# A mixture-of-experts stage on one core: first w1 pieces of the next expert ahead of w2, the first group gathered whole, the last expert in full rows

## The chip, the cores and the metric

The kernel runs on one core of one Trainium2 chip. The metric is device time in microseconds: the median of three runs. A separate execution was taken with the hardware profiler; its span (first to last instruction) and its own time are given below.

## The reference, cut to what matters

One layer of a hybrid backbone over 256 latent tokens of width 1024: modulated norm, one input projection, differential attention and a long convolution, a gated merge, an output projection; then a mixture of 32 experts, of which each token takes 4. The change touches the end of the output projection and the experts:

```python
x_new = x + g1 * merge_branches(oa, ob, gx, *merge_params)
x_new = x_new + g2 * moe_ffn(modulate(x_new, norm2_g[l], sh2, sc2), *moe_params)

# moe_ffn: route, then for each block of rows of one expert e
logits = (xt @ router_w + router_b)
top_v, top_i = lax.top_k(logits, 4)
wts = softmax(top_v)
gu = xblk @ w1[e] + b1[e]               # w1[e]: 1024 x 2048
gate, up = split(gu, 2)
gate = min(gate, 7); up = clip(up, -7, 7)
act = (up + 1) * gate * sigmoid(1.702 * gate)
y = act @ w2[e] + b2[e]                 # w2[e]: 1024 x 1024, added with wts to its tokens
```

All weights are float32: an expert is 8 MB of w1 and 4 MB of w2, the 32 experts 403 MB, of 467 MB that the DMA queues move.

## The kernel before, in words

**Loads.** All weights go through one list of loads of 1 MiB (`want`), in the order of use, each into one of 25 slots of 8 KB per partition (`NS`). SyncE issues the next load when a slot is free and the number of loads held is under a bound; the bound follows a table of steps (`ROOM`), where a step is any taking or giving back of a slot (`tick`). `done(key)` gives a used piece's slot back. Slots also hold arrays: X (the new rows), XN (their normed rows, split into a high and a low float32r part), RAW (quarters, here the gathered columns of four experts), YS (outputs of two experts), MTh/MTl (the merged branches split in two), PAIR. At the start of the experts 24 loads may be held; then the bound falls to 20.

**Order.** Instructions of each engine run in the order in which the program writes them. In the projections, steps of other work are hung on numbered weight pieces (`TASKS`): `bias_load` and `bias_parts` bring the experts' first bias in and split it (ACT casts, POOL subtractions), `merge_a` writes MTh on ACT and MTl on POOL for the output projection, whose pieces are 96 to 111.

**Between projection and experts.** `new_rows` adds the projection to x (VectorE); `squares` and `rstd` make the norm's factor; `new_columns`, `logits`, `folded`, `top4` and `positions` do the routing. `spin` runs a few idle matmuls.

**Experts.** Slots of 64 rows per expert. `gather(g)` makes the columns of four experts in four steps k2 of two column blocks: a one-hot matrix S (`slots_of`) times both parts of XN, then scale and shift on ACT and VectorE (`modulate_slots`) into RAW. Group 0 is different: `gather_first` makes expert 0 alone from X in float32, one step per piece of w1, so that XN and RAW are allocated after w1 of expert 0; the other three of the group follow after its w2. For each expert `up_bias` starts the two PSUM sums, `up` runs the eight pieces of w1 (four matmuls each, gate and up, two column halves), `hidden` does clamp, sigmoid and product on VectorE and ACT, and `down` transposes the hidden layer, copies it (`at`), runs w2 (four loads), and writes the output in two parts to YS (`yr`, `YS`). Between `up` and the transposes stand `up_bias` of the next expert, on even experts `scatter` of the pair before (one-hot times YS, added to X), at expert 1 `second_bias`, and at the end of each group the next gather and its `weights`.

**The last expert** (31) is loaded in halves of hidden columns: w1 in rows of 256 columns (1 KB), each load of two pieces, w2 in rows of 512 columns. `up_last(q)`, `last_units(q)` and `down_last(q, c)` work half by half; `out_rows` and `scatter_last` write the result by column halves c and row tiles i. The scatter of expert 30 (`last_but_one`), its weights and G2 are hung between pieces (`between`).

Scratch tiles of 2 KB per partition (`t1_tile`) take four tags in turn; one is kept for the second part of the first bias.

Of the kernel before, what the change touches and what calls it, by code (L numbers as in the profile page):

```python
# [20 lines left out]
P = 128  # L21
# [50 lines left out]
    ("bias_load", (), (90,)), ("merge_b", (1, 1), (90,)), ("merge_a", (0, 0), (93, 94)), ("merge_a", (0, 1), (95, 97)), ("bias_parts", (), (99,)),  # L72
# [17 lines left out]
]  # L90

# [62 lines left out]
def tile_kernel(ctx: ExitStack, tc: tile.TileContext, a: dict, out: bass.AP):  # L154
# [140 lines left out]
    for h in range(4):  # L295
        want(("out", h), [P, 2, 1024], a["w_out"][0, h * 256:(h + 1) * 256].rearrange("(k p) n -> p k n", p=P))
        PIECES += [(("out", h), j) for j in range(4)]
    for e in range(NE - 1):
        for k in range(KC):
            want(("w1", e, k), [P, 2048], a["exp_w1"][0, e, k * P:(k + 1) * P, :])  # L300
# [5 lines left out]
    w2 = a["exp_w2"][0, NE - 1].rearrange("(b f p) n -> p b f n", p=P, b=2)  # L306
    for q in range(2):
        for k in range(0, KC, 2):
            want(("w1", NE - 1, q, k), [P, 2, 4, 256], [(j, w1[:, k + j, :, q * 256:(q + 1) * 256]) for j in range(2)])
    for q in range(2):  # L310
        for c in range(2):
            want(("w2", NE - 1, q, c), [P, 2, 2, 512], [(b, w2[:, b, 2 * q:2 * q + 2, c * 512:(c + 1) * 512]) for b in range(2)])
# [83 lines left out]
    T1 = deque(range(4))  # L396

    def t1_tile(shape, name, dt=F32):
        T1.rotate(-1)
        return wk.tile(shape, dt, tag=f"t1{T1[-1]}", name=name, bufs=1)  # L400

# [36 lines left out]
    Z = t1_tile([P, 512], "Z")  # L438
# [7 lines left out]
    cT = t1_tile([P, KC, 32], "cT")  # L446
# [15 lines left out]
    def bias_parts():  # L462
        B1.append(kept([P, 512], "B1", F32R))
        B1.append(t1_tile([P, 512], "B1u", F32R))
        T1.pop()
# [349 lines left out]
    def qk_rope(raw, rstd, gain, rt, nm):  # L815
        r3 = raw.rearrange("p (g f) -> p g f", g=8)
        t1 = t1_tile([P, 512], f"t1{nm}")
# [221 lines left out]
    def pt_out(h, i):  # L1039
        e2 = es.pop((h, i))[0]  # L1040
        if i == 0:
            PTs[h] = [t1_tile([P, 2, T], f"PT{h}{j}") for j in range(2)]
# [264 lines left out]
    def new_rows(i, h):  # L1307
        hs = slice(h * 512, (h + 1) * 512)
        t_ = t1_tile([P, 512], f"og{i}{h}")
# [65 lines left out]
    def up_bias(e, q=""):  # L1375
        g, u = pst(f"ps_eg{e}{q}", True), pst(f"ps_eu{e}{q}", True)
        acts[e, q] = g, u
        cols = slice(0, 512) if q == "" else slice(q * 256, q * 256 + 256)
        for b, ps in ((0, g), (1, u)):
            pe.matmul(ps[:, 0:cols.stop - cols.start], pick, B1[b][:, cols], start=True, stop=False, skip_group_check=True)  # L1380
        if q != 0 and e < NE - 1:
# [3 lines left out]
    for i in range(2):  # L1385
# [5 lines left out]
        if i == 0:  # L1391
            squares(0)
    free.extend(ring)
    tick("arrays", -3)
    release("MTl", "MTh")
    new_columns(0, (act.copy, act.copy))
    spin(SPINS[5])
    new_columns(1, (dve.tensor_copy, act.copy))
    squares(1)
    logits(0)  # L1400
    rstd(0)
# [3 lines left out]
    rstd(1)  # L1405
    for i in range(2):
# [4 lines left out]
    for i in range(2):  # L1411
        positions(i)
    spin(SPINS[8])

    SS, XG, OT = {}, {}, {}
    XN = []


    def rows_parts():
        hi_, lo_ = XN  # L1420
        for i in range(2):
            act.activation(hi_[:, i], X[:, i], AF.Copy, scale=st2[:, i, 5:6])
            dve.scalar_tensor_tensor(lo_[:, i], X[:, i], st2[:, i, 5:6], hi_.bitcast(F32)[:, i], ALU.mult, ALU.subtract)

# [13 lines left out]
    first = []  # L1438

    def gather_first(k):  # L1440
        if k == 0:
            first.extend((t1_tile([P, KC, CAP], "xg0"), pst("ps_xg0", True),
                          wk.tile([P, 2, CAP], F32, tag="hz", name="S0", bufs=3)))
            for i in range(2):
                dve.tensor_scalar(first[2][:, i], iota, pos[:, i, 0:1], st2[:, i, 5:6], ALU.is_equal, ALU.mult)
        xg, ps, s0 = first
        for i in range(2):
            pe.matmul(ps[:, k * CAP:(k + 1) * CAP], X[:, i, k * P:(k + 1) * P], s0[:, i], start=(i == 0), stop=(i == 1))
        modulate_slots(xg[:, k], ps[:, k * CAP:(k + 1) * CAP], k, act if k % 2 else dve)
        XG[0, k] = xg[:, k]  # L1450
        if k == KC - 1:
            unhold("ps_xg0")

    def gather(g):
        n = 4 if g else 3
        for k2 in range(4):
            xg = quarter([P, 2, 4, CAP], F32)
            ps = pst(f"ps_xg{g}_{k2}")
            for kk in range(2):
                k = 2 * k2 + kk  # L1460
                for j, (i, xn) in enumerate((i, xn) for i in range(2) for xn in XN):
                    pe.matmul(ps[:, kk * T:(kk + 1) * T], xn[:, i, k * P:(k + 1) * P],  # L1462
                              SS[g][:, i].rearrange("p e c -> p (e c)"), start=(j == 0), stop=(j == 3))
            for kk in range(2):
                k = 2 * k2 + kk
                modulate_slots(xg[:, kk, 4 - n:4].rearrange("p e c -> p (e c)"), ps[:, kk * T + (4 - n) * CAP:(kk + 1) * T], k, dve if kk else act)
                for e in range(4 - n, 4):
                    XG[4 * g + e, k] = xg[:, kk, e]
# [32 lines left out]
    def up(e):  # L1501
        g, u = acts.pop((e, ""))
        for k in range(KC):
            wt = w(("w1", e, k))
            xg = XG[e, k]
            for b, ps in ((0, g), (1, u)):
                for h in range(2):
                    pe.matmul(ps[64 * h:64 * h + 64, :], xg, wt[:, b * 1024 + h * 512:b * 1024 + (h + 1) * 512],  # L1508
                              start=False, stop=(k == KC - 1), skip_group_check=True)
            done(("w1", e, k))  # L1510
            if e == 0 and k < KC - 2:
                gather_first(k + 2)
# [294 lines left out]
```

## Time and profile before

| | |
|---|---|
| median of three runs | 1273.14 us (1270.09 to 1273.43) |
| profiled execution | 1275.61 us, span 1273.9 us |
| TensorE | 1119.0 us busy (88%), mean granted clock 0.969 of 2.4 GHz |
| VectorE, ACT, POOL | 514.0, 279.3, 167.4 us busy |
| DMA | 467.10 MB, mean 367 GB/s |
| chain that ended last | TensorE 43%, DMA 35%, VectorE 13% |

The page cuts the span into 40 slices of 31.8 us. TensorE's busy share is high nearly everywhere, but its matmuls overlap and their ends are modelled, so that row alone does not say what bounds the kernel; the rows on what the DMA engines moved, and the chain of waits, say more.

### The profile page before, as it was taken

Reading aid. Unit: us, or ns where it says so; the run is one execution under the profiler, and the core shown is the slowest. Engines: PE = TensorE matmul, PEld = TensorE weight load, DVE = VectorE, ACT = ScalarE, POOL = GpSimd, SP = SyncE. Lnnn points to the kernel's source line nnn. Section 1 sums busy time; section 2 is a strip of 40 time slices with the busy share of each in tenths; the row PEclk is TensorE's granted clock in tenths of the full one; section 3 lists DMA queues with packets and bytes.
Section 4 is the critical chain, followed back from the end, with each engine's and each line's share of the span. In section 5 each row is a group of like instructions: output and inputs, shape, how many; then the busy total and the mean of one; then the engine's idle time right before and its main releaser. Section 6 shows DMA issues by size and latency. Waiting matters only on the chain.

```text
span 1273.9 us, 14261 instructions
## 1 busy us (share of the span) xinstructions
PE 1119.0 (88%) x5645; PEld 551.6 (43%) x5645; DVE 514.0 (40%) x817; ACT 279.3 (22%) x506; POOL 167.4 (13%) x152
## 2 busy tenths in 40 slices
PE   7889789998889899989989888888888798879896
PEld 5678678896333433333343224222322332233232
DVE  5699995966222322232323123322312322223232
ACT  5563465753210101011111001111100101111110
POOL 2385454322000000000000000000000000000000
PEclk9999899999889899999989999999999999999999
DMA  9984536878689999999999999999999999999996
GB/s 328 400 289 153 181 130 234 328 303 351 261 319 415 387 384 416 417 418 418 417 417 417 416 417 417 417 417 417 418 417 418 417 417 418 417 418 417 418 371 238
DMA packets 105810, 467.10 MB, mean 367 GB/s; under 512 B 8992, under 2 KB 18188, under 8 KB 71948
## 3 DMA queue, kind: packets, MB, share of 16 engines
q1 hardware_dynamic: 102416, 462.26, 90.8%
q10 hardware_dynamic: 3324, 3.88, 1.0%
q8 instruction: 46, 0.75, 0.2%
q14 instruction: 24, 0.20, 0.0%
HBM read 465.07 MB, written 1.05 MB: 366 GB/s over the span
## 4 chain that ended last, share of the span: by engine, by line
PE 43%; DMA 35%; DVE 13%; ACT 3%; issue 3%; POOL 2%; ACTq 0%; SPq 0%; DVEq 0%; POOLq 0%
PE ps_ey L1540 12%; PE ps_eg L1508 9%; PE ps_eu L1508 9%; PE ps_xg L1462 2%; DMA w____w___22___3__5783<-in_exp_w_dram 2%; DVE AA L643 2%; DMA w____w___16___3__5011<-in_exp_w_dram 2%; DMA w____w___29___3__6656<-in_exp_w_dram 2%; DMA w____w___14___3__4793<-in_exp_w_dram 2%; DMA w___w___29__3__6520<-in_exp_w_dram 2%; DMA w___w___27__3__6302<-in_exp_w_dram 2%; DMA w____w___25___3__6161<-in_exp_w_dram 2%; DMA w___w___15__7__4862<-in_exp_w_dram 2%; DMA w____w___20___3__5506<-in_exp_w_dram 2%; DMA w____w___27___3__6379<-in_exp_w_dram 2%
## 5 line engine op out<-in xcount | busy, mean ns | idle before, releaser
L1520 DVE TENSOR_SCALAR ga<-ps_eg 128x512 f32<-128x512 f32 (+1 forms) x33 | 22.3, 675 | 325.9 <-PE ps_eg L1508 318.4
L481 POOL CAST pick<-both 128x128 fp32r<-128x128 f32 x32 | 24.5, 766 | 862.1 <-PE ps_eu L1380 862.0
L1554 DVE TENSOR_TENSOR yr<-ps_ey,G 64x512 f32<-64x512 f32 x62 | 42.7, 688 | 229.0 <-PE ps_ey L1540 228.3
L1555 ACT ACTIVATE YS<-yr,wsl 64x512 fp32r<-64x512 f32 x62 | 44.6, 719 | 311.8 <-DVE yr L1554 311.8
L1521 ACT ACTIVATE sg<-ga 128x512 f32<-128x512 f32 (+1 forms) x33 | 20.4, 619 | 352.9 <-DVE ga L1520 352.9
L1556 DVE SCALAR_TENSOR_TENSOR YS<-yr,wsl,YS 64x512 fp32r<-64x512 f32 x62 | 46.3, 747 | 48.8 <-ACT YS L1555 48.8
L1462 PE MATMUL ps_xg<-S,XNh 128*128 128x256 f32 x128 | 37.3, 324 | 13.9 <-DVE S L1429 13.9
L1665 DVE TENSOR_TENSOR X<-X,ps_sc 128x512 f32<-128x512 f32 x60 | 37.4, 680 | 3.0 <-PE ps_sc L1663 3.0
L392 PE MATMUL ps_g<-XTh,wsp 128*128 128x256 f32 x128 | 37.9, 296 | 0.0
L393 PE MATMUL ps_g<-XTl,wsp 128*128 128x256 f32 x128 | 36.2, 283 | 0.0
L394 PE MATMUL ps_g<-XTh,wsp 128*128 128x256 f32 x128 | 36.2, 283 | 0.0
L1462 PEld LDWEIGHTS ps_xg<-S,XNh 128*128 128x128 f32 x128 | 28.6, 223 | 17.2 <-DVE S L1429 17.0
L1462 PE MATMUL ps_xg<-S,XNl 128*128 128x256 f32 x128 | 35.9, 312 | 0.0
L1535 ACT COPY at<-ps_at 128x512 f32<-128x512 f32 x31 | 18.2, 586 | 78.9 <-PE ps_at L1533 78.9
L1533 PE MATMUL ps_at<-ident,ua 128*128 128x128 f32 x124 | 20.6, 291 | 13.8 <-DVE ua L1525 13.4
L1660 PE MATMUL ps_sc<-YS,OT 128*128 128x512 f32 x120 | 30.9, 395 | 0.0
L1462 PEld LDWEIGHTS ps_xg<-S,XNl 128*128 128x128 f32 x128 | 28.6, 224 | 0.0
L1434 DVE TENSOR_SCALAR RAW<-ps_xg,s,sh 128x256 f32<-128x256 f32 (+1 forms) x32 | 16.9, 534 | 25.8 <-ACT RAW L1436 25.8
L1522 DVE TENSOR_SCALAR ua<-ps_eu 128x512 f32<-128x512 f32 (+1 forms) x33 | 22.3, 675 | 10.7 <-PE ps_ey L1624 5.5
L1436 ACT ACTIVATE RAW<-ps_xg,sh,s 128x256 f32<-128x256 f32 (+1 forms) x32 | 17.5, 556 | 37.4 <-PE ps_xg L1462 37.4
L392 PEld LDWEIGHTS ps_g<-XTh,wsp 128*128 128x128 f32 x128 | 24.4, 191 | 2.7 <-issue 2.2
L1660 PEld LDWEIGHTS ps_sc<-YS,OT 128*128 128x128 f32 x120 | 22.2, 188 | 7.1 <-issue 2.3
(1792 smaller groups left out, 2461.7 us busy)
## 6 DMA issues: line engine op xcount, KB each, us to landing
w_x<-in_x_dram SPq DMA_DIRECT2D x2, 512.0 KB, 4.8
w___ada___0__0__88<-in_ada_w_dram SPq DMA_DIRECT2D x2, 512.0 KB, 7.3
w___ada___0__1__91<-in_ada_w_dram SPq DMA_DIRECT2D x2, 512.0 KB, 10.4
w___ada___0__2__95<-in_ada_w_dram SPq DMA_DIRECT2D x2, 512.0 KB, 10.5
w___ada___0__3__98<-in_ada_w_dram SPq DMA_DIRECT2D x2, 512.0 KB, 12.3
w___in____q___0__101<-in_w_in_dram SPq DMA_DIRECT2D x2, 512.0 KB, 12.3
w___in____h___0__104<-in_w_in_dram SPq DMA_DIRECT2D x1, 1024.0 KB, 12.4
w___ada___1__0__108<-in_ada_w_dram SPq DMA_DIRECT2D x2, 512.0 KB, 11.6
```

What stands on the lines that cost most here:

```text
L392: pe.matmul(ps, ahi, bhi, start=start, stop=False, **kw)
L393: pe.matmul(ps, ahi, blo, start=False, stop=False, **kw)
L394: pe.matmul(ps, alo, bhi, start=False, stop=stop, **kw)
L643: dve.scalar_tensor_tensor(ada_ps[g][:, hs], wt[:, hs], col[:, k:k + 1], ada_ps[g][:, hs], ALU.mult, ALU.add)
L1462: pe.matmul(ps[:, kk * T:(kk + 1) * T], xn[:, i, k * P:(k + 1) * P], SS[g][:, i].rearrange("p e c -> p (e c)"), start=(j == 0), stop=(j == 3))
L1508: pe.matmul(ps[64 * h:64 * h + 64, :], xg, wt[:, b * 1024 + h * 512:b * 1024 + (h + 1) * 512], start=False, stop=(k == KC - 1), skip_group ...
L1540: pe.matmul(yp[64 * h:64 * h + 64, :], at[:, f % 4, f // 4], wt[:, f % 2, h * 512:(h + 1) * 512], start=(f == 0), stop=(f == KC - 1))
L1554: dve.tensor_tensor(raw, yp[64 * h:64 * h + 64, :], G2[64 * h:64 * h + 64, :], ALU.mult)
L1555: act.activation(hi_[r, cs], raw, AF.Copy, scale=wsl[r, pr:pr + 1])
L1556: dve.scalar_tensor_tensor(lo_[r, cs], raw, wsl[r, pr:pr + 1], hi_.bitcast(F32)[r, cs], ALU.mult, ALU.subtract)
L1660: pe.matmul(ps, OT[pr][:, i], YP[pr][j][:, h * 512:(h + 1) * 512], start=(j == 0), stop=(j == 1 and pr > 0))
L1665: dve.tensor_tensor(xs, xs, ps, ALU.add)
```

## The change: what it does

1. The loads of w1 of the next expert come in two parts: pieces 0 to 2 (`LEAD = 3`) ahead of w2 of this expert, pieces 3 to 7 behind it. TensorE uses them in that order: pieces 0 and 1 before the transposes of the hidden layer, piece 2 behind them, then w2.
2. XN is allocated and written between projection and routing, RAW before the first gather; group 0 is gathered whole, steps 0 and 1 ahead of w1 of expert 0, steps 2 and 3 between its pieces. `gather_first` goes. `ROOM` allows 21 loads at the start and 20 once YS stands. `rstd(0)` stands right behind the new rows.
3. The last expert has w1 in full rows (loads like all others) and w2 in four chunks by column half c and hidden half q.
4. `bias_parts` is hung on piece 103 instead of 99. The scratch tiles become one pool of four buffers.

```diff
-    ("bias_load", (), (90,)), ... ("bias_parts", (), (99,)),
+    ("bias_load", (), (90,)), ... ("bias_parts", (), (103,)),
...
-    (102, 14), ... (118, 18), (122, 21), (123, 22),
-    (124, 23), (125, 24), (131, 23), (132, 22), (133, 21), (140, 20), (501, 19), ...
+    (102, 14), ... (118, 18), (122, 21), (136, 20),
+    (501, 19), ...
+LEAD = 3
...
+    def want_up(e, ks):
+        for k in ks:
+            want(("w1", e, k), [P, 2048], a["exp_w1"][0, e, k * P:(k + 1) * P, :])
+    want_up(0, range(KC))
     for e in range(NE - 1):
-        for k in range(KC):
-            want(("w1", e, k), [P, 2048], ...)
+        want_up(e + 1, range(LEAD))
         for h in range(4):
             want((("w2", e), h), ...)
-    w1 = a["exp_w1"][0, NE - 1].rearrange("(k p) (b n) -> p k b n", p=P, b=4)
-    ...
-            want(("w1", NE - 1, q, k), [P, 2, 4, 256], [(j, w1[:, k + j, :, q * 256:(q + 1) * 256]) for j in range(2)])
-    ...
-            want(("w2", NE - 1, q, c), [P, 2, 2, 512], ...)
+        want_up(e + 1, range(LEAD, KC))
+    for c in range(2):
+        for q in range(2):
+            want(("w2", NE - 1, q, c), [P, 4, 512], w2[:, q, :, c * 512:(c + 1) * 512])
...
+    rstd(0)
     free.extend(ring)
     tick("arrays", -3)
     release("MTl", "MTh")
+    XN = [alloc([P, 2, 1024], f"XN{j}", F32R) for j in "hl"]
+    def row_hi(i, h):   # ACT: XN high part, half a row tile
+    def row_lo(i, h):   # VectorE: XN low part
     new_columns(0, (act.copy, act.copy))
+    row_hi(0, 0)
     spin(SPINS[5])
     new_columns(1, (dve.tensor_copy, act.copy))
     squares(1)
+    row_hi(0, 1)
+    row_lo(0, 0)
     logits(0)
-    rstd(0)
     logits(1)
     release("PAIR")
     spin(SPINS[6])
     rstd(1)
+    row_hi(1, 0)
+    row_hi(1, 1)
...
         positions(i)
+    row_lo(1, 0)
     spin(SPINS[8])
...
-    gather_first(0)
-    gather_first(1)
+    cut("RAW", 4)
     slots_of(0)
-    for e in range(NE - 1):
-        ga = up(e)
-        ...
-        down(e, ga)
-        if e == 0:
-            cut("RAW", 4)
-            gather(0)
-    up_last(0)
-    up_last(1)
-    ...
+    row_lo(0, 1)
+    row_lo(1, 1)
+    for k2 in range(4):
+        gather(0, k2)
+        if k2:
+            up(0, (2 * k2 - 2, 2 * k2 - 1))
+    routing_weights()
+    act.activation(warm, onesf, AF.Sigmoid)
+    up(0, (6, 7))
+    for e in range(NE):
+        if e:
+            up(e, range(LEAD, KC))
+        ua = hidden(e)
+        if e == 0:
+            YS.append(alloc([P, 2, 1024], "YS", F32R))
+        if e < NE - 1:
+            up_bias(e + 1)
+        if e % 2 == 0 and e:
+            scatter(e // 2 - 1)
+        if e == 1:
+            second_bias()
+        g = e // 4 + 1
+        if e % 4 == 3 and e < NE - 1:
+            slots_of(g)
+            for k2 in range(4):
+                gather(g, k2)
+        elif e < NE - 1:
+            up(e + 1, range(LEAD - 1))
+        at = units(e, ua)
+        if e == NE - 1:
+            break
+        if e % 4 == 3:
+            weights(g)
+            up(e + 1, range(LEAD - 1))
+        elif e == 0:
+            weights(0)
+        up(e + 1, (LEAD - 1,))
+        down(e, at)
+    ...
+    down_last(at, 0, 0)
+    down_last(at, 1, 0)
     out_rows(0)
-    down_last(1, 1, (0,))
+    down_last(at, 0, 1)
     scatter_last(0, 0)
-    down_last(1, 1, (1,))
+    scatter_last(0, 1)
+    down_last(at, 1, 1)
     out_rows(1)
-    for c, i in ((0, 1), (1, 0), (1, 1)):
-        scatter_last(c, i)
+    scatter_last(1, 0)
+    scatter_last(1, 1)
```

`units` is the first half of the old `down` (transposes and copy), `down` the rest. In `between`, the last scatter's steps of expert 30 move to the pieces 4 to 7 of expert 31.

## Rows read from the trace of the kernel before

**Rows 1.** The page: what DMA moved, in 40 equal slices.
```profile
GB/s 328 400 289 153 181 130 234 328 303 351 261 319 415 387 384 416 417 418 418 417 417 417 416 417 417 417 417 417 418 417 418 417 417 418 417 418 417 418 371 238
```
**Rows 2.** The chain that ended last, in order of time: start us, us, what.
```profile
723.01 20.14 DMA w____w___14___3__4793<-in_exp_w_dram
```
**Rows 3.** Busy us of PE, PEld, DVE, ACT, POOL; granted clock, DMA share, GB/s.
```profile
336.00:348.00 12.00, 8.36 (x28) 2.63 (x26) 7.00 (x16) 4.99 (x7) 0.30 (x1) 0.72 0.10 31
...
480.00:1216.00 736.00, 643.85 (x2908) 233.91 (x2904) 200.14 (x313) 81.69 (x128) 20.53 (x25) 0.98 1.02 417
```
**Rows 4.** The same columns, the stretch to the plateau and the last expert's.
```profile
310.00:480.00 170.00, 153.67 (x684) 62.70 (x684) 49.71 (x103) 25.97 (x44) 5.34 (x9) 0.91 0.89 357
...
1224.00:1249.00 25.00, 22.41 (x144) 10.04 (x142) 7.31 (x12) 2.23 (x4) 0.00 (x0) 1.00 1.06 346
1249.00:1260.00 11.00, 7.48 (x42) 2.28 (x38) 1.70 (x4) 0.42 (x1) 0.00 (x0) 1.00 0.98 361
```
**Rows 5.** Timeline of SyncE: start us, us, line, the load issued.
```profile
306.39 0.33 SPq L327 DMA_DIRECT2D w___w___1__7__2961<-in_exp_w_dram  x1
...
330.55 0.33 SPq L327 DMA_DIRECT2D w___w___2__4__3120<-in_exp_w_dram  x1
345.85 0.33 SPq L327 DMA_DIRECT2D w___w___2__5__3185<-in_exp_w_dram  x1
...
360.10 0.38 SPq L327 DMA_DIRECT2D w____w___2___0__3272<-in_exp_w_dram  x1
```
**Rows 6.** DMA issues: the load, count, KB each, us from issue to landing.
```profile
w___w___1__7__2961<-in_exp_w_dram SPq DMA_DIRECT2D x1, 1024.0 KB, 8.0
...
w___w___2__5__3185<-in_exp_w_dram SPq DMA_DIRECT2D x1, 1024.0 KB, 4.8
```
**Rows 7.** Waits of TensorE and POOL's work, output projection (timeline; idle and releaser last).
```profile
293.19 0.50 PE L392 MATMUL ps_out<-wsp,MTh 128*128 128x512 f32 x1 [0.64 <-ACT MTh L1244]
...
295.64 0.50 PE L394 MATMUL ps_out<-wsp,MTl 128*128 128x512 f32 x1 [1.72 <-POOL MTl L1245]
...
288.58 1.65 POOL L469 TENSOR_TENSOR B<-b,B 64x512 fp32r<-64x512 f32 x1
```
**Rows 8.** VectorE and ACT from the new rows to the routing (timeline).
```profile
307.13 0.69 DVE L1312 TENSOR_TENSOR X<-X,og 128x512 f32<-128x512 f32 x1
...
306.84 1.07 ACT L1333 COPY PAIR<-ps_xt 128x512 f32<-128x512 f32 x2 [0.93 <-PE ps_xt L1332]
...
313.65 0.19 DVE L1371 SCALAR_TENSOR_TENSOR pos<-mskb,ps_pos 128x32 f32<-128x32 bf16 x1 [0.29 <-PE ps_pos L1370]
```
**Rows 9.** The chain, in order of time: TensorE's pieces of w1 and w2, a gather.
```profile
317.03 1.91 PE ps_eg L1508 x4
...
409.00 7.09 PE ps_ey L1540 x32
...
424.67 0.86 PE ps_eg L1508 x4
...
543.61 4.15 PE ps_xg L1462 x32
```
**Rows 10.** Stretches with their granted clock (columns as in rows 3).
```profile
864.00:896.00 32.00, 23.92 (x120) 9.55 (x116) 9.77 (x18) 4.55 (x8) 0.82 (x1) 1.00 1.02 418
314.00:320.00 6.00, 5.56 (x20) 2.99 (x19) 1.30 (x5) 0.40 (x1) 0.00 (x0) 0.50 1.03 418
```
**Rows 11.** The chain, in order of time: the experts 30 and 31.
```profile
1216.65 1.08 PE ps_eg L1508 x4
...
1222.88 7.11 PE ps_ey L1540 x32
...
1260.74 2.80 PE ps_ey L1624 x12
...
1265.61 2.79 PE ps_last L1631 x6
1268.42 0.69 DVE X L1633
```

More of the change, by code (lines that the diff above doesn't have):

```diff
@@ L1041, in pt_out @@
         if i == 0:
-            PTs[h] = [t1_tile([P, 2, T], f"PT{h}{j}") for j in range(2)]
+            PTs[h] = [wk.tile([P, 2, T], F32, tag="t1", name=f"PT{h}{j}", bufs=4) for j in range(2)]
         ps = pst(f"ps_p{h}{i}", True)
@@ L1373, in tile_kernel, with up_bias @@
     acts = {}
[L1375 to L1381, printed above, removed]
+    def up_bias(e):
+        acts[e] = pst(f"ps_eg{e}", True), pst(f"ps_eu{e}", True)
+        for b, ps in enumerate(acts[e]):
+            pe.matmul(ps, pick, B1[b], start=True, stop=False, skip_group_check=True)
+        if e < NE - 1:
             pick_rows(e + 1)
@@ L1412, in tile_kernel @@
         positions(i)
+    row_lo(1, 0)
     spin(SPINS[8])
     SS, XG, OT = {}, {}, {}
[L1416 to L1423, printed above, removed]
     def slots_of(g):
@@ L1436, in modulate_slots, with gather @@
             act.activation(o, ps, AF.Identity, bias=sh2[:, k:k + 1], scale=s2[:, k:k + 1])
[L1438 to L1468, printed above, removed]
+    def gather(g, k2):
+        xg = quarter([P, 2, 4, CAP], F32)
+        ps = pst(f"ps_xg{g}_{k2}")
+        for kk in range(2):
+            k = 2 * k2 + kk
+            for j, (i, xn) in enumerate((i, xn) for i in range(2) for xn in XN):
+                pe.matmul(ps[:, kk * T:(kk + 1) * T], xn[:, i, k * P:(k + 1) * P],
+                          SS[g][:, i].rearrange("p e c -> p (e c)"), start=(j == 0), stop=(j == 3))
+        for kk in range(2):
+            k = 2 * k2 + kk
+            modulate_slots(xg[:, kk].rearrange("p e c -> p (e c)"), ps[:, kk * T:(kk + 1) * T], k, dve if kk and (g or k2) else act)
+            for e in range(4):
+                XG[4 * g + e, k] = xg[:, kk, e]
     cmaxi = kept([P, 1], "cmaxi", I32)
@@ L1608, in last_units @@
-    def last_units(q):
-        e, ua = NE - 1, last["ua", q]
-        ps = pst(f"ps_at{e}{q}")
-        for c in range(2):
-            pe.transpose(ps[:, c * P:(c + 1) * P], ua[:, c * P:(c + 1) * P], ident)
-        at = t1_tile([P, 4, 2, CAP], f"at{e}{q}")[:, 0:2]
-        act.copy(at.rearrange("p c h s -> p (c h s)"), ps[:, 0:2 * P])
-        if not q:
-            last["y"] = [pst(f"ps_ey{e}{c}", True) for c in range(2)]
-        last["at", q] = at
-    def down_last(q, c, bs=(0, 1)):
-        yp, at = last["y"][c], last["at", q]
-        for b in bs:
-            for f in range(2):
-                r = slice(64 * f, 64 * f + 64)
-                pe.matmul(yp[r], at[:, f, b], w(("w2", NE - 1, q, c))[:, b, f], start=(q == 0 and b == 0), stop=(q == 1 and b == 1))
+    between = {(NE - 2, 3): lambda: last_g2(0), (NE - 2, 4): lambda: last_g2(1), (NE - 2, 5): lambda: last_weights(0),
+               (NE - 2, 6): lambda: last_weights(1),
+               **{(NE - 1, 4 + 2 * i + c): lambda i=i, c=c: last_but_one(i, c) for i in range(2) for c in range(2)}}
@@ L1626, in out_rows, with down_last @@
+    def down_last(at, q, c):
+        e, yp = NE - 1, last["y", c]
+        wt = w(("w2", e, q, c))
+        for f in range(2):
+            for j in range(2):
+                pe.matmul(yp[64 * j:64 * j + 64], at[:, 2 * j + f, q], wt[:, 2 * j + f], start=(q == 0 and f == 0), stop=(q == 1 and f == 1))
     def out_rows(c):
-        dve.tensor_tensor(last["Y"][c], last["y"][c], last["g2", c], ALU.mult)
+        dve.tensor_tensor(last["Y"][c], last["y", c], last["g2", c], ALU.mult)
     def scatter_last(c, i):
```

105 lines of the change are left out of this document (31 added, 74 removed), and 6 rows, old and new, of the table ROOM.

## The prediction

> **What bounds the kernel now.** The slices of the page come first [rows 1]: fifteen ragged slices, then from the sixteenth (478 us) a plateau of 416 to 418 GB/s that breaks only in the last two. The chain of waits says what the plateau is: from 723 us on most of it is transfers of 20 us, one behind the other, the first of them in [rows 2], and the sum by stretches has 417 GB/s over all of 480 to 1216 us with TensorE busy 644 of 736 us [rows 3]. So the expert stage is one stream of 1 MiB loads, 2.51 us each (1.0486 MB at 417 GB/s), 30.2 us per expert. What happens on TensorE there costs nothing while the stream never stops. Three things set the end: how much the stream has lost before it is steady, how fast it runs at its end, and what follows its end.
>
> The loss before: from 310 to 480 us the mean is 357 GB/s [rows 4], so 170 x (1 - 357/417) = 24.5 us of transfer time were not used. The largest hole is plain, 31 GB/s from 336 to 348 us [rows 3]; a second stands near 358, a small one near 440. SyncE's issues say why [rows 5]: a load at 330.55, the next at 345.85, two more, and then none until 360.10. A load is issued when a slot comes free; all slots hold landed pieces, and TensorE waits for the hidden layer of expert 0, then works on its w2 and on the first gather, in which few or none come free.
>
> **The change, part by part.** *Fewer slots, a later first release.* The split rows XN take two slots before the experts start and RAW a third, so 21 loads are held at the start, not 24. All 21 are issued by 307 us as now. The load issued at 306.39 + 0.33 lands 8.0 us later [rows 5, 6], at 314.7; one more follows, so the stream runs dry at 317.2 by landings. It starts again when the first piece of w1 has been used.
>
> When is that? Now it is 320.7 (the matmuls from 317.03 run until then, and the issue behind them restarts the flow). Four shifts. (a) The bias parts go from piece 99 to 103, so POOL has no five casts and subtractions (from 288.58) ahead of the last low part of the merge. TensorE waited 0.64 + 1.72 us for its two halves [rows 7]. I take 2.0 of these 2.4 us back; the bounds are 0.7 (ACT's half can be no earlier) and 2.4. The parts then run beside output matmuls that wait for neither. (b) The first square root now stands on ACT ahead of the column copies, and waits for VectorE's last new rows, which end at 307.82, and three small operations: about 308.6 where the copies now start at 306.84 [rows 8]. With two row casts of 0.6 us in the same queue, one in a gap of that length, the routing ends 2.0 us later: 315.8 for 313.8. (c) Behind it VectorE has one low part (0.75) and the slots (0.76) before the first gather may start: 317.3. (d) Two of the four gather steps precede the first w1 piece. A whole gather takes 4.15 us [rows 9], so two take 2.1, or 3.6 if the clock is at 1.2 GHz, as it now is from 314 to 320 us, after a stretch of short waits (granted 0.50) [rows 10]; the first piece takes 1.9 at 2.4 GHz, 3.6 at 1.2 (its first half 1.91 [rows 9]). With a clock that rises inside this stretch I get 323.7, less (a): 321.7. Bounds: 318.9 (all fast, 2.4 back) to 325.3 (all slow, 0.7 back, and the gather waiting for the other two low parts, 1.5).
>
> A load issued into an empty queue lands 4.8 us after issue [rows 6], so the 22nd lands at 321.7 + 0.4 + 4.8 = 326.9. The stream ran dry at 317.2 - 2.0 = 315.2 and would have gone on in steps of 2.51: 9.2 us lost, of which (a) has paid 2.0. Net 7.2.
>
> *No holes after it.* This needs releases to keep ahead of 2.51 us per load. After the first release at t, the rest of w1 of expert 0 at 1.72 us a piece (twice 0.86 [rows 9]) with two gather steps of 1.0 between gives releases up to t + 12.5 (seven loads; the eighth slot goes to YS). Then the new order matters: two pieces of expert 1 run while VectorE and ACT do the hidden layer (t + 16.6 and 18.3), a third behind the transposes (21.4), the four of w2 at 1.77 (7.09 for all four [rows 9]) up to 28.2, and on without a pause. The nth new load lands at t + 5.2 + 2.51(n - 1) if nothing is late; a release plus 5.2 must be no later. The eighth has 1.0 us in hand, the tenth 1.2, and then slack grows, because releases come every 1.72. At expert 1 the transposes for the second bias now stand ahead of the moved pieces and wait some 3 us for VectorE's hidden layer; five loads (12 us) are then in flight. The scatter of expert 2 and the gather behind expert 3 (some 11 us without a release) meet a backlog of about 19 us. So the hole of 336 to 348 closes by the moved pieces, the one near 358 by the gather that is already done, the one of 440 by the lead. Gain 24.5 - 7.2 = **17.3 us** (13.7 to 20.1 by the bounds, 3 less if the slim margins break). The moved loads keep their order equal to that of use, so SyncE's queue has no head that waits for a later user. Per expert TensorE needs 13.8 + 7.1 and some 3 us for bias, transposes, scatter and gather, 24 of 30.2, so it catches up and then waits for the stream, as now from 723 us: sixteen loads of lead at 362 us, less 2.5 per expert, are gone near 520 us. That this comes sooner is worth nothing. The scratch tiles of the hidden layer turn over three buffers in both kernels (the fourth keeps the second bias), and the next user stands 8.6 us of w1 behind; I cost that edit at nothing, and a wait there would have to pass those 8.6 us to count.
>
> *The last expert.* The piece that ends w1 of expert 30 lands at 1216.6 and its matmuls follow at once [rows 11]; in both orders the same loads stand before it. Now 57.3 us remain. In this stretch w1 of expert 31 comes in rows of 1 KB, at 346 GB/s [rows 4]: 8.39 MB in 24.2 us instead of 20.1. The Trainium skill, "DMA: Bandwidth & Descriptors", section Specifications, asks only for transfers of 512 B or more for line rate, by which these rows would lose nothing and this part's gain would shrink by 4.1 us; the row of this trace has them 17% slower.
>
> After the change 12 loads of full rows follow that piece until w1 of expert 31 is in: 30.2 us. From its landing: 6.2 us until w2 may start, as at expert 30 (1216.6 to 1222.88 [rows 11]), and 1.4 for the two matmuls and the addition of the last scatter of expert 30 that now stand ahead of the hidden layer. Then four chunks of w2 at 0.93 (2.80 for three), four scatters at 0.93 (2.79 for three) and one product on VectorE (0.7) in line: 7.6 + 1.9 + 0.9 + 1.9 + 0.9 + 0.7 + 1.9 = 15.8, by when the last chunk (four loads, 10 us, 11.6 at the 361 GB/s of 2 KB rows [rows 4]) has long landed. From the last addition to the end takes 5.5 (1268.42 to 1273.9). Sum 21.3, and 1.0 for a clock that may fall in the 3.6 us in which TensorE waits for the hidden layer (0 to 3.4). 30.2 + 22.3 = 52.5: gain **4.8 us** (2.4 to 5.8).
>
> Sum: 17.3 + 4.8 = 22.1, so a span of 1251.8 for 1273.9. The profiled execution took 1275.6, 1.7 more than its span; the runs have a median of 1273.14 (1270.09 to 1273.43), and against that I forecast 1251.
>
> **The rivals.** *Hidden anyway* (0.13): the early holes only move. The three slots fewer cost 7.5 us, the first release is late, and if the margins of 1 us break at every pause, the early gain is about zero and the last stage's 4.8 remain: 1268. For it: those margins, and 20 slots in both kernels once YS stands. Against: TensorE's two long pauses without releases are gone by construction, and pieces come at 1.72.
>
> *Rows of 1 KB were not the brake* (0.08): 4.1 us less, 1255. For it: at its end the stream also has an SP queue that issues pieces in twos. Against: the w2 rows of 2 KB, also in twos, have 361, between the two.
>
> *The clock* (0.05, the slower side). The new order parts each expert's w1 run in two, with waits of 0.6 to 0.8 us at every piece once the stream leads. If TensorE is granted 1.2 GHz for half of the stage, its 24 us per expert become 32, the stream is no longer the bound, and some 23 experts lose 1.8 us each: 1251 + 42 = 1293; it decides from about 0.41 of the time at the low level. Against: with TensorE busy 23.9 of 32 us the stretch from 864 is granted 1.00 [rows 10], and the plateau as a whole 0.98 [rows 3]; such waits are there today. The Trainium skill, "TensorE: Matmul & The Clock Gate", section on HAM oscillation, says that a thin loop which waits for a DMA between its pieces is throttled again and again, and wants them run together; here it would speak for this rival, and those rows differ from it.
>
> **How the numbers follow.** Forecast 0.70, its own range 1247 to 1260 (gains of 13.7 - 3 to 20.1 and of 2.4 to 5.8, added); 0.04 is for what I do not see. The range of 1243 to 1266 holds the second rival too, goes most of the way to the first, and leaves 4 us below. What can be told from no change is 0.3%, 1269.3 to 1277. Faster 0.89: forecast, second rival, and most of the first; same 0.05; slower 0.06.
>
> **What would show it.** After: no stretch under 380 GB/s between 330 us and the last 25 us, but one hole of 8 to 11 us between 313 and 326; 21 loads issued by 306; the first w1 release near 322; the chain made of transfers from about 520 us on, not 723; w1 of expert 30 in at 1199; 417 GB/s while w1 of expert 31 comes. I am wrong if a second hole stands near 340 us, if the granted clock of the plateau is under 0.9, or if the last transfer of w1 lands more than 23 us before the end.

## The result, and the profile after

The changed kernel takes 1258.87 us (median, 1258.50 to 1262.86) against 1271.85 for the kernel before in the same comparison: ratio 0.9905, 95% interval [0.9880, 0.9931]. A second comparison gave 1257.43 against 1270.99, 0.9892 [0.9875, 0.9909]. It is faster, by 13 us or 1%; the forecast was 1251, a gain of 22.1. The profiled execution took 1259.04 us, its span is 1257.3.

What DMA moved in 40 slices of the page of after, to be read against [rows 1]:

```profile
GB/s 334 400 294 150 191 110 230 332 296 354 322 413 417 418 416 418 417 418 417 417 417 416 417 416 417 417 417 417 417 418 418 417 416 418 418 418 417 417 416 172
```

The plateau begins in the twelfth slice (346 us) instead of the sixteenth (478 us), and it holds up to the last slice. The stretches of after, with the columns of [rows 3] (busy us of PE, PEld, DVE, ACT, POOL; granted clock, DMA share, GB/s):

```profile
290.00:297.00 7.00, 6.66 (x30) 5.20 (x29) 4.88 (x7) 4.28 (x9) 5.85 (x5) 1.00 0.77 286
310.00:336.00 26.00, 24.07 (x119) 11.50 (x119) 9.80 (x34) 7.64 (x13) 1.12 (x2) 0.93 0.70 270
336.00:348.00 12.00, 12.00 (x60) 4.36 (x58) 2.17 (x6) 0.59 (x1) 0.00 (x0) 1.00 1.02 422
310.00:480.00 170.00, 162.46 (x753) 63.30 (x753) 50.94 (x98) 24.26 (x40) 6.67 (x10) 0.98 0.97 394
480.00:1200.00 720.00, 623.84 (x2798) 218.09 (x2796) 195.98 (x307) 79.57 (x125) 19.38 (x24) 0.99 1.02 417
1207.00:1232.00 25.00, 21.98 (x92) 6.24 (x90) 4.93 (x7) 2.03 (x3) 0.00 (x0) 1.00 1.02 409
1232.00:1243.00 11.00, 6.68 (x22) 2.54 (x22) 3.27 (x5) 1.22 (x2) 0.00 (x0) 0.69 0.47 178
```

Behind 310 us there is one hole, in 310 to 336: 26 x (1 - 270/417) = 9.2 us, the forecast's figure. 336 to 348 has 422 GB/s where [rows 3] has 31. From 310 to 480 the loss is 170 x (1 - 394/417) = 9.4 us for 24.5 [rows 4]. While w1 of expert 31 comes (1207 to 1232, with the first rows of its w2) it is 409 for 346 [rows 4]. The last row covers the wait for the last hidden layer and what follows: the granted clock is 0.69 on average, which is 1.2 GHz for 6.8 of 11 us.

The chain that ended last, of after, in order of time (start, us, what):

```profile
563.16 20.47 DMA w___w___10__3__4181<-in_exp_w_dram
...
1199.39 1.08 PE ps_eg L1493 x4
...
1230.23 1.01 PE ps_eg L1493 x4
1236.35 1.10 PE ps_at L1513 x4
1238.16 7.41 PE ps_ey L1582 x24
1245.57 1.92 PE ps_last L1589 x4
1247.48 1.89 PE ps_ey L1582 x8
1250.15 2.00 PE ps_last L1589 x4
```

The last w1 piece of expert 30 is used at 1199.39 us, 17.3 before [rows 11], to a tenth as forecast. But from there to the end it takes 1257.3 - 1199.4 = 57.9 us, where the kernel before takes 57.3 and the forecast had 52.5. The early term came in, in this pair of executions; the last stage's 4.8 us did not. TensorE's timeline in that stage says where they are (idle time and releaser last):

```profile
1236.35 1.08 PE L1513 MATMUL ps_at<-ident,ua 128*128 128x128 f32 x4 [3.59 <-DVE ua L1507]
...
1238.16 3.68 PE L1582 MATMUL ps_ey<-w___w___31__0__0__6824,at 128*64 128x512 f32 x8 [0.73 <-ACT at L1515]
...
1241.63 2.23 PE L1582 MATMUL ps_ey<-w___w___31__1__0__6830,at 128*64 128x512 f32 x8
...
1243.69 1.88 PE L1582 MATMUL ps_ey<-w___w___31__0__1__6836,at 128*64 128x512 f32 x8
```

One chunk of w2 has eight records (the x8 at the end of a line) and takes 1.88 us at 2.4 GHz, not 0.93; and behind the wait of 3.59 us the transposes take 1.08 us and the first chunk 3.68, both at 1.2 GHz.

### The profile page after: what moved, and what is told of

Read it like the earlier page. It is cut to its first block, busy times and chain, and to the rows that moved or that the text cites. A ratio compares the mean times of both kernels' runs of the same rounds, so it can differ in the third digit from the quotient of the medians.

```text
span 1257.3 us, 14035 instructions
## 1 busy us (share of the span) xinstructions
PE 1110.7 (88%) x5547; PEld 535.7 (43%) x5547; DVE 509.3 (41%) x808; ACT 277.2 (22%) x503; POOL 167.4 (13%) x152
## 4 chain that ended last, share of the span: by engine, by line
DMA 48%; PE 34%; DVE 11%; issue 2%; ACT 2%; POOL 1%; ACTq 0%; SPq 0%; DVEq 0%; POOLq 0%
PE ps_eg L1493 8%; PE ps_eu L1493 7%; PE ps_ey L1525 6%; PE ps_xg L1448 2%; DMA w___w___22__3__5666<-in_exp_w_dram 2%; DMA w___w___10__3__4181<-in_exp_w_dram 2%; DMA w___w___13__7__4620<-in_exp_w_dram 2%; DMA w___w___11__7__4343<-in_exp_w_dram 2%; DMA w___w___20__7__5450<-in_exp_w_dram 2%; DMA w___w___12__3__4399<-in_exp_w_dram 2%; DMA w___w___28__7__6440<-in_exp_w_dram 2%; DMA w____w___27___0__6355<-in_exp_w_dram 2%; DMA w____w___29___0__6632<-in_exp_w_dram 2%; DMA w___w___19__3__5288<-in_exp_w_dram 2%; DMA w___w___23__7__5828<-in_exp_w_dram 2%
## 5 line engine op out<-in xcount | busy, mean ns | idle before, releaser
L1502 DVE TENSOR_SCALAR ga<-ps_eg 128x512 f32<-128x512 f32 x32 | 22.1, 691 | 162.2 <-PE ps_eg L1493 162.2
L1503 ACT ACTIVATE sg<-ga 128x512 f32<-128x512 f32 x32 | 20.2, 632 | 215.0 <-DVE ga L1502 215.0
L1438 DVE TENSOR_SCALAR RAW<-ps_xg,s,sh 128x256 f32<-128x256 f32 x31 | 16.9, 544 | 36.9 <-ACT RAW L1440 36.9
L1440 ACT ACTIVATE RAW<-ps_xg,sh,s 128x256 f32<-128x256 f32 x33 | 18.5, 564 | 50.7 <-PE ps_xg L1448 50.7
L397 PEld LDWEIGHTS ps_g<-XTh,wsp 128*128 128x128 f32 x128 | 24.5, 191 | 2.7 <-issue 2.2
L1618 PEld LDWEIGHTS ps_sc<-YS,OT 128*128 128x128 f32 x120 | 22.3, 188 | 7.2 <-issue 2.3
L398 PEld LDWEIGHTS ps_g<-XTl,wsp 128*128 128x128 f32 x128 | 24.5, 191 | 0.1
L399 PEld LDWEIGHTS ps_g<-XTh,wsp 128*128 128x128 f32 x128 | 24.5, 191 | 0.0
```

What stands on the lines that cost most here:

```text
L397: pe.matmul(ps, ahi, bhi, start=start, stop=False, **kw)
L398: pe.matmul(ps, ahi, blo, start=False, stop=False, **kw)
L399: pe.matmul(ps, alo, bhi, start=False, stop=stop, **kw)
L1618: pe.matmul(ps, OT[pr][:, i], YP[pr][j][:, h * 512:(h + 1) * 512], start=(j == 0), stop=(j == 1 and pr > 0))
```

## The experiments

Theory A: the early part gave its 17 us, the last stage gave nothing, because TensorE's chain behind the last w1 piece was priced too short and runs partly at the low clock. Theory B: the last stage gave its 4.8 us and the rest was lost elsewhere in the stream. "The stage" below is the time from the first use of the last w1 piece of expert 30 to the end of the span; a run's time is a median, its stage is read from its one profiled execution.

**Each part alone.** The early part, with the last expert as before:

```diff
-    for e in range(NE):
+    for e in range(NE - 1):      # no piece of expert 31 ahead
...
+    up_last(0)
+    up_last(1)                   # and the old last_units, down_last, order of scatters
```

> The kernel after the change with the last expert of the kernel before (w1 in 1 KB rows, halves of columns, w2 in its old chunks), and with no piece of expert 31 used ahead. Theory A (the early part gave its 17.3 us whole, the new last stage gave nothing: 57.9 us from the landing of the last w1 piece of expert 30 to the end, against 57.3 before): that piece is in at 1199.4 us as after the change, 57.3 remain, span 1256.7, 0.6 us under the 1258.9 of the kernel after. Theory B (the last stage did give its 4.8 us, and the missing 9 us were lost elsewhere in the stream): span near 1262, time near 1263.7.

The last expert alone, on the kernel before:

```diff
-            want(("w1", NE - 1, q, k), [P, 2, 4, 256], ...)
+        want(("w1", NE - 1, k), [P, 2048], a["exp_w1"][0, NE - 1, k * P:(k + 1) * P, :])
...
-    up_last(0)
-    up_last(1)
+    ua = up(NE - 1)              # then the new transposes, down_last, order of scatters
```

> The kernel before with the last expert of the kernel after (w1 in full rows, one hidden layer, w2 in column-half chunks), all before it left as it was. Theory A: the last w1 piece of expert 30 is in at 1216.7 as before and 57 to 59 us remain, 1271 to 1274, no difference from before that can be measured. Theory B: 52.5 us remain, 1267.

The early part alone takes 1257.34 us (0.9884 [0.9859, 0.9909]), the last part alone 1269.62 (0.9987 [0.9968, 1.0005]). The first is 14.7 us under the 1272.01 of its comparison, so it holds all of the gain; the second can't be told from no change. B falls, and A holds in the main: the second run is 1.4 us under A's range of 1271 to 1274 and 2.6 over B's 1267, and its stage was 55.9 us where A had 57 to 59 and B 52.5. The first run's stage was 54.7. While w1 of expert 31 comes, the first kernel (rows of 1 KB) has 350 GB/s and the second (full rows) 418; one window of each:

```profile
1207.00:1232.00 25.00, 23.10 (x154) 10.49 (x150) 7.32 (x12) 2.23 (x4) 0.00 (x0) 1.00 1.07 350
```

```profile
1213.00:1238.00 25.00, 22.09 (x98) 7.64 (x96) 8.58 (x13) 2.66 (x4) 0.00 (x0) 1.00 1.02 418
```

So the stream's part of the forecast's last term did arrive, and was spent behind it. Counted from the use of the last w1 piece of expert 30, the last one of expert 31 is used after 30.1 us in the second run and 30.8 in the kernel after, but after 33.8 in the first run and 35.0 in the kernel before, here from its timeline:

```profile
1251.67 0.65 PE L1600 MATMUL ps_eg<-w___w___31__1__6__6849,RAW 128*64 128x256 f32 x4 [0.40 <-DMA w___w___31__1__6__6849<-in_exp_w_dram]
```

From there to the end the old order took 22.2 us in the kernel before and 20.9 in the first run, the new order 27.1 in the kernel after and 25.8 in the second run. The full rows gave 4 us, and the chain behind them took as much.

**The rows.** The forecast gave rows of 1 KB a price, and had a rival that they have none. To free it from the place at the end, 32 loads in the middle of the plateau were cut in two, once into rows of 1 KB and once of 4 KB:

```diff
-            want(("w1", e, k), [P, 2048], a["exp_w1"][0, e, k * P:(k + 1) * P, :])
+            want(("w1", e, k), [P, 2048], ... if e not in (12, 13, 14, 15) else
+                 tuple(....rearrange("p (b n) -> p b n", b=4)[:, :, q * 256:(q + 1) * 256] for q in range(2)))
...              # the run with 4 KB:
+                 tuple(a["exp_w1"][0, e, k * P:(k + 1) * P, q * 1024:(q + 1) * 1024] for q in range(2)))
...              # and one DMA for each of the two
```

> The kernel after the change, with the 32 loads of w1 of experts 12 to 15 each issued as two DMAs of 512 KB in rows of 1 KB (the four blocks of 256 columns of one half of the columns), as w1 of the last expert was before; all else is unchanged. Theory A (rows of 1 KB run at 346 GB/s wherever they stand): 32 x (1.0486 MB / 346 - 1.0486 / 417) = 16.5 us later, 1275.4, and some 346 to 360 GB/s in about 100 us of the plateau, the w2 loads between them at 417. Rival (it was the end of the stream that was slow, not its rows): under 2 us, 1259 to 1261, and 410 GB/s throughout.

> As the run with rows of 1 KB, but the two DMAs of each of the 32 loads take rows of 4 KB (one half of the columns, unbroken). Theory A (the length of the row is the brake): 1258 to 1260 and 417 GB/s, no change. Rival (loads issued in twos are the brake, and the rows of 1 KB only came along with it): about as late as the run with rows of 1 KB.

1274.99 us with rows of 1 KB (1.0034 [1.0018, 1.0049]), 1259.77 with rows of 4 KB (0.9899 [0.9871, 0.9927]). With 1 KB the last w1 piece of expert 30 is used at 1215.32 instead of 1199.39: 15.9 us for 32 loads, 0.50 each, so 3.01 us for 2.51, or 348 GB/s. Two windows of that kernel, with w2 loads among the w1 loads:

```profile
640.00:700.00 60.00, 46.68 (x202) 14.86 (x198) 13.67 (x20) 4.72 (x7) 1.30 (x2) 1.00 1.09 361
700.00:752.00 52.00, 38.81 (x166) 12.35 (x166) 10.66 (x16) 4.68 (x7) 0.81 (x1) 1.00 1.07 371
```

and the same with 4 KB:

```profile
640.00:700.00 60.00, 54.13 (x234) 16.21 (x230) 13.66 (x20) 5.31 (x8) 1.32 (x2) 1.00 1.03 409
700.00:752.00 52.00, 42.50 (x174) 12.15 (x175) 14.33 (x22) 4.72 (x7) 1.64 (x2) 1.00 1.03 411
```

It is the length of the row, not the place and not the two halves. The 1 to 2% that are missing to 417 belong to rows of 4 KB too: in the kernel after the w2 loads have such rows, each load in one DMA, and the stretch in which they pass has the same rate:

```profile
690.00:698.00 8.00, 6.75 (x30) 2.06 (x32) 0.00 (x0) 0.59 (x1) 0.00 (x0) 1.00 1.02 410
```

The rival falls. The Trainium skill, "DMA: Bandwidth & Descriptors", section Specifications, asks for 512 B or more for line rate; here rows of 1 KB have 17% less, and the measurement decides.

**The pieces moved ahead.** The lead set to nothing:

```diff
-LEAD = 3
+LEAD = 0
...
-        up(e + 1, (LEAD - 1,))
         down(e, at)
```

> The kernel after the change with no piece of the next expert's w1 loaded or used ahead of w2 (the lead is 0 instead of 3); the whole first gather, the split rows and the last expert stay as changed. Theory as the forecast's sentence has it (the hole of 336 to 348 us closes by the moved pieces): a hole of 8 to 11 us comes back near 335 to 350 us, w1 of expert 30 is in at 1208 to 1210, time 1267 to 1270. Rival (it is the gather and the split rows, no longer standing between w1 and w2 of expert 0, that close it): the pause of releases is 7 us against 20 loads in flight or landed, a hole of 2 to 3 us at most, time 1259 to 1262.

1262.95 us (0.9923 [0.9898, 0.9949]), 4.1 over the kernel after (5.5 over its second median): between the theory and the rival, nearer to the rival. Its windows and SyncE's issues:

```profile
336.00:348.00 12.00, 10.23 (x44) 3.56 (x42) 4.72 (x8) 1.22 (x2) 0.82 (x1) 0.86 0.75 293
348.00:364.00 16.00, 16.00 (x77) 5.20 (x73) 3.56 (x5) 1.50 (x3) 0.00 (x0) 1.00 1.01 401
310.00:480.00 170.00, 155.85 (x737) 62.69 (x737) 52.37 (x104) 27.79 (x48) 6.65 (x10) 0.96 0.95 384
```

```profile
336.08 0.33 SPq L332 DMA_DIRECT2D w___w___2__3__3172<-in_exp_w_dram  x1
344.93 0.33 SPq L332 DMA_DIRECT2D w___w___2__4__3216<-in_exp_w_dram  x1
```

No slot comes free for 8.9 us, and 12 x (1 - 293/417) = 3.6 us are lost there. In the kernel before it was 12 x (1 - 31/417) = 11.1 [rows 3]. So the moved pieces close a third of that hole. The other 7.5 us close through the rest of the early change; that it is the split rows and the whole gather, which no longer stand between w1 and w2 of expert 0, is argued from the order, not tested alone. (This kernel's profiled execution was 3.6 us longer than its median, most of it lost ahead of 290 us.)

**The clock in the last wait.**

```diff
+        if e == NE - 1:
+            spin(14)
         at = units(e, ua)
```

> The kernel after the change with 14 idle 128x128 matmuls on TensorE in the 3.6 us in which it waits for the last hidden layer; they take about 3 us there and feed nothing. Theory A (the fall of the clock to 1.2 GHz from 1235.5 us, for 6.8 us, costs 3 us: 0.4 in the transposes, 1.8 in the first chunk, 0.35 in the second and the rest in their ends): granted clock 1.00 from 1232 to 1245, 55 us from the last w1 piece of expert 30 to the end instead of 57.9, time 1256. Rival (the chain is held by landings of w2 or by the other engines, not by TensorE's clock): the clock stays up and the stage still takes 57 to 58 us, time 1258 to 1259.

1256.26 us (0.9875 [0.9854, 0.9897]), stage 54.9. The same stretch of the last stage, and TensorE's timeline:

```profile
1231.00:1242.00 11.00, 10.09 (x60) 5.55 (x58) 3.96 (x6) 1.22 (x2) 0.00 (x0) 1.00 0.51 192
```

```profile
1231.91 3.39 PE L487 MATMUL ps_spin<-ident 128*128 128x128 f32 x28
...
1235.48 0.66 PE L1513 MATMUL ps_at<-ident,ua 128*128 128x128 f32 x4 [0.18 <-DVE ua L1507]
...
1236.87 1.94 PE L1582 MATMUL ps_ey<-w___w___31__0__0__6824,at 128*64 128x512 f32 x8 [0.73 <-ACT at L1515]
```

Clock 1.00, the transposes 0.66 us for 1.08, the first chunk 1.94 for 3.68, the second 1.89 for 2.23. The stage is 3.0 us shorter, and 2.5 of these lie behind the use of the last w1 piece of expert 31 (24.6 us to the end for 27.1): that is what the low clock cost, where the forecast allowed 1.0. The medians differ by 2.6 us, and by 1.2 from the second one of the kernel after; their intervals overlap, so the price rests on the traces.

**The order, and halves.** The last two scatter steps of expert 30 behind the hidden layer:

```diff
-               **{(NE - 1, 4 + 2 * i + c): lambda i=i, c=c: last_but_one(i, c) ...}
+               **{(NE - 1, 4 + c): lambda c=c: last_but_one(0, c) for c in range(2)}}
...
+            last_but_one(1, 0)
+            last_but_one(1, 1)
+            spin(4)
         at = units(e, ua)
```

> The kernel after the change with the last two scatter steps of expert 30 (matmuls and additions) put behind the last hidden layer instead of among the last pieces of w1, and 4 idle matmuls after them. Theory A (after the last w1 piece the chain on VectorE and TensorE sets the end): the hidden layer starts 1.3 us earlier, the clock holds as with the 14 idle matmuls, 53.6 us from the last w1 piece of expert 30 to the end instead of 57.9 (54.9 with the idle matmuls alone), time 1254.5 to 1255. Rival (w2's landings set it by now): 54.9 as before, time 1256.

1254.89 us (0.9872 [0.9849, 0.9895]), stage 53.0: w2 starts 5.6 us after the use of the last w1 piece of expert 31, with the idle matmuls alone 7.5. The 1.9 us are VectorE's, which takes the hidden layer at once, with no addition ahead of it (1.3 were expected). Then the hidden layer in two halves of columns, in two orders of what follows:

```diff
+        for s in cols:           # two halves of 256 columns
+            dve.tensor_scalar(ua[:, s], u[:, s], 7.0, -7.0, ALU.min, ALU.max)
+            dve.scalar_tensor_tensor(...); dve.tensor_tensor(...)
...
+    units_half(NE - 1, ua, 0)
...
+    down_last(at, (0,), 0)       # second run; the first: down_last(at, 0, 0)
+    units_half(NE - 1, ua, 1)
```

> As the run before this one, and the last hidden layer goes in two halves of 256 columns, so that the transposes and half of the first column half of w2 run beside VectorE's second half; the two rows of the array pair over the two halves of w2's rows, and 8 idle matmuls stand in the waits. Theory A: TensorE starts w2 about 2.5 us earlier than with the order alone and then meets the landing of the last w2 chunk near 1240.3 us: 1.9 us for it, and 7.9 from there to the end, 50.7 us from the last w1 piece of expert 30, time 1251.5 to 1253. Rival (half the columns cost nearly as much per instruction, and the waits only multiply): 53 to 54 us, no faster than the order alone, time 1254.5 to 1256.

> The last stage in two halves of the hidden layer as in the run with halves, but w2 of both column halves goes without a break, the transposes of the second half stand behind the first row block, and the four last scatters come after all of w2, so that the first two hide the product on VectorE. Theory (TensorE's chain: 30.1 us to the start of the last w1 piece, 4.5 to the start of w2, 7.4 + 0.4 for w2 and transposes, 0.4 for a landing, 4.0 for the scatters, 0.9 for the last addition, 5.1 to the end): 52.8 us or a little less, against 54.8 with the first order of halves and 53.0 with the whole hidden layer, time 1254 to 1255. Rival (the scatters of the first column half now delay its stores, and the end waits for four stores at once): 54 to 55 us, 1256.

1256.99 us (0.9880 [0.9856, 0.9905]) with a stage of 54.8, and 1255.27 (0.9872 [0.9851, 0.9893]) with 55.7: in the stage both theories missed, by 4.1 and 2.9 us, and the rivals were nearer, though not for the reasons they gave. (The time of the second is near both its theory and its rival.) In the first, the first column half of w2 takes 5.5 us for 3.8, with a wait for its second chunk (0.64 on the weight load) and one for the copy of the second half. In the second, w2 starts 4.5 us after the last w1 piece, as expected, and then TensorE waits:

```profile
1239.82 0.64 PE L1601 MATMUL ps_ey<-w___w___31__1__1__6850,at 128*64 128x512 f32 x1 [1.43 <-DMA w___w___31__1__1__6850<-in_exp_w_dram]
```

The halves pair the two row blocks of w2, so that 3.7 us of matmuls stand behind the landing of the very last chunk; in the order of the changed kernel only one chunk, 1.9, does. The next limit of this stage is that landing, 42.1 us after the last w1 piece of expert 30; with the order alone the last chunk starts at 43.0. Why it lands so late was not tested. In the kernel after, SyncE's issue of the chunk ahead of it takes 9.27 us, so that the last one is issued only then:

```profile
1217.62 9.27 SPq L332 DMA_DIRECT2D w___w___31__0__1__6836<-in_exp_w_dram  x1
1226.98 2.39 SPq L332 DMA_DIRECT2D w___w___31__1__1__6850<-in_exp_w_dram  x1
```

The version with the order and the few idle matmuls has the lowest median of those run; its interval overlaps those of the changed kernel and of the second run with halves, but its stage is 4 to 5 us shorter in the trace than the changed kernel's.

**The size of the early term.** The kernel before, profiled again; the kernel after, again; and the kernel after with the bias parts at their old place (`("bias_parts", (), (99,))`):

> The kernel before, unchanged, in a second profiled execution. Theory A (the profiled execution on which the forecast was worked out was a long one: 1275.6 against a median of 1272 in 17 runs, with 74.7 MB loaded at 300 us where the other kernels have 75.9 to 76.2, and 60.5 MB from 310 to 480 us): 75.5 to 76.2 MB at 300 us, 61.5 to 62.5 MB from 310 to 480 us, the last w1 piece of expert 30 in at 1211 to 1214, and 54.5 to 57.5 us from there to the end. Rival (that execution was typical, and the early part of the change gives 17 us against every run): 74.7 MB, 60.5 MB and 1216 to 1217.

> The kernel after, unchanged, again, to be compared with the two others of this call on the same chip: 1258 to 1260, ratio to before 0.989 to 0.991; 57 to 58 us from the last w1 piece of expert 30 to the end, the clock low for 3.4 or 6.8 us from the wait for the last hidden layer on. If the 5 us that are missing in the last stage were an accident of one profile, this stage takes 53 us here.

> The kernel after with the bias parts back at piece 99, where the kernel before has them. Forecast's term (a): TensorE waits for two halves of the last low part again, the release that follows comes 2.0 us later (0.7 to 2.4), and the stream stands still for as long near 290 us: 165 to 200 GB/s in 290 to 297 us instead of 286, 1260 to 1261.5. Rival (the wait is hidden by loads in flight): no difference, 1259.

The second profile of before has 75.0 MB moved by the queue of loads at 300 us, less than expected, but from 310 to 480 us:

```profile
310.00:480.00 170.00, 153.67 (x727) 63.30 (x717) 51.20 (x108) 27.08 (x47) 5.33 (x9) 0.95 0.91 368
```

368 GB/s for 357 [rows 4], 4.5 us less lost, and the last w1 piece of expert 30 at 1212.9. With the last expert alone changed (all ahead of it as before) it was 1211.8. The three profiles of the old early part thus have 1213.8 on average, and the seven of the new one, with nothing changed up to there, 1195.3 to 1201.4, on average 1198.7: a gain of 15.0, not 17.3. The old stage, 57.3 in the first profile, was 59.4 in the second and 54.7 with the early part alone; the new one was 57.9 and 57.0, and 58.0, 58.2 and 57.3 in the three runs that leave it as it is (the two on rows and the one below). The two differ by less than they vary. Part of that is the clock: in the second profile of before it fell to 1.2 GHz for 3.4 us soon after a wait of 1.68 us, a wait that stands in the first profile too, and the chunk that takes 1.94 us in the first profile took 3.24:

```profile
1257.03 3.24 PE L1624 MATMUL ps_ey<-w___w___31__1__0__6878,at 128*64 128x512 f32 x8 [0.51 <-ACT at L1614]
```

The run with the early bias parts took 1262.84 (0.9923 [0.9897, 0.9949]). From 310 to 480 us it equals the kernel after (395 GB/s), in 290 to 297 it has

```profile
290.00:297.00 7.00, 4.88 (x21) 3.40 (x19) 6.97 (x8) 3.26 (x6) 6.76 (x7) 1.00 0.52 181
```

for 286, which is 7 x 105/417 = 1.8 us, near the forecast's 2.0. Its waits on TensorE settle the term: the two of [rows 7] are back, where the kernel after has one of 0.34 us (last line), so 2.0 us are the moved step's:

```profile
294.78 0.50 PE L397 MATMUL ps_out<-wsp,MTh 128*128 128x512 f32 x1 [0.62 <-ACT MTh L1242]
297.22 0.55 PE L399 MATMUL ps_out<-wsp,MTl 128*128 128x512 f32 x1 [1.72 <-POOL MTl L1243]
...
292.64 0.50 PE L399 MATMUL ps_out<-wsp,MTl 128*128 128x512 f32 x1 [0.34 <-POOL MTl L1243]
```

But this execution was already 1.0 MB (2.3 us) behind at 286 us, ahead of the moved step, so the 4.0 us by which its time is longer (5.4 against the median of the same comparison) are not that step's alone.

## Why the prediction was right on the early stream and 8 us short

**The early stream: right, and its size is that of one execution.** The forecast's 17.3 us is what the two profiles show. The steps behind it held too: 21 loads were issued by 304.2 us, the stream ran dry, and the first release came at 319.0, for 321.7. SyncE in after:

```profile
303.78 0.42 SPq L332 DMA_DIRECT2D w___w___2__0__2967<-in_exp_w_dram  x1
318.99 0.33 SPq L332 DMA_DIRECT2D w___w___2__1__3100<-in_exp_w_dram  x1
```

What ran dry earlier also started earlier, so the hole is the same 9.2 us. The new rows end at 304.82 for 307.82 [rows 8]; by bytes this execution was 0.8 us ahead at 286 us, so some 2.2 are left for term (a), which the waits have at 2.0. The square root stands 0.5 us behind them, where (b) had 0.8, and the gather starts at 313.34, two us ahead of the sum (317.3 less 2.0):

```profile
304.13 0.69 DVE L1310 TENSOR_TENSOR X<-X,og 128x512 f32<-128x512 f32 x1
...
305.31 0.20 ACT L1322 ACTIVATE st<-st 128x1 f32<-128x1 f32 x1 [2.40 <-DVE st L1321]
...
313.34 0.36 PE L1448 MATMUL ps_xg<-S,XNh 128*128 128x256 f32 x1 [0.60 <-DVE S L1433]
```

But the term was worked out against one execution, 1275.6 us, and subtracted from a median. That execution had lost more than the others of its kernel: the gain over the average of three is 15.0. So 2.3 us of the missing 9 are the yardstick's.

**A reason within it was wrong.** "So the hole of 336 to 348 closes by the moved pieces": it closes by a third through them. The forecast gave the gather that is already done only the hole near 358, and did not price the two apart.

**The last expert: the step that failed.** "30.2 us" until w1 of expert 31 is in was right (30.8 to its use), with the full rows at 409 to 418 GB/s. "Then four chunks of w2 at 0.93 (2.80 for three)" was not: the 2.80 of [rows 11] are twelve records, which the forecast read as three chunks of four. A chunk has eight: it takes 1.88, and four of them 3.8 us more than the sum has. "1.0 for a clock that may fall" was 2.5. Against that the last addition to the end took 5.1, not 5.5. From w1's last piece to the end it is 27.1 us where the forecast had 22.3; 4.8 us short (3.8 + 1.5 - 0.4, and -0.1 of small terms), which is the whole of the term. The sentence that this would be wrong "if the last transfer of w1 lands more than 23 us before the end" is what happened. The sum also shows why nothing is left of the 4 us of the full rows: with the clock held the new order still needs 24.6 us behind w1 where the old one needed 20.9 and 22.2, because the old one had half of the transposes and of w2 done under the stream; the rest is the clock.

**The rivals.** *Hidden anyway* fell: 394 GB/s in 310 to 480. *Rows of 1 KB were not the brake* fell by the pair of runs. *The clock* fell: 0.99 over the plateau (0.98 before), so the broken runs of w1 did not throttle it. The loop of which the Trainium skill tells ("TensorE: Matmul & The Clock Gate", HAM oscillation) waits longer for its DMA than the matmuls between two waits take; here most waits of the plateau were of 0.5 to 0.6 us against 1.72 of matmuls per piece, so it did not speak for this rival, as the forecast had it, and these rows are no test of it. From 480 us on the granted clock fell four times: for 3.4 us at 515, 751 and 993 us, each time in a gather behind a wait of 1.99 us, and for 6.8 us ahead of the last transposes. The chain is made of transfers from 563 us, not 520, worth nothing as said.

The sum: 15.0 for the early part and about nothing for the last, against 13.0 and 13.6 measured; 1 to 2 us are within the spread of the runs.

## What to carry to other kernels

When a duration is read from a chain that groups records, divide by the records and count those of the new step; a factor of two in the tail cost this forecast 3.8 us, more than any of its doubtful terms. A stage that ends a kernel is a chain, so ask of the old order what it hid before pricing the new one, and give a long wait on TensorE the price of what follows it at 1.2 GHz: here 2.5 us behind a wait of 3.59. Profile the kernel before more than once if terms of a few us are worked out from one execution.

## What the runs showed of the hardware

Executions of the same instructions up to some 286 us had moved between 70.6 and 73.4 MB by then on the queue of loads (the kernel with a lead of 0, and the one with the order changed), 6.7 us of stream; most have their slots full near 290 us (73.7 MB), and there a part of that is taken back. Rows of 1 KB run at 348 GB/s and rows of 4 KB at about 410, also in mid-stream, where the plateau (w1 in rows of 8 KB, w2 in rows of 4 KB) has 417. An idle stretch of 3.59 us ahead of the last transposes stands in seven executions: in six the transposes ran at 1.2 GHz (1.08 or 1.09 us) and the clock stayed there for 6.8 us, in the seventh (the last part alone) they still ran at 2.4 (0.63) and the clock fell behind them for 3.4. Idle matmuls in its place kept 2.4.
